# Even rows of x handed over transposed, their norm applied at eviction, odd rows transposed once on chip

## The chip, the cores and the metric

The kernel runs on one core of a Trainium2 chip. The metric is the device time of one execution in microseconds, the median over runs. The engines are TensorE (PE, whose weight loads are listed as PEld), VectorE (DVE), ScalarE (ACT), GpSimd (POOL) and SyncE (SP), which here issues the DMAs. Work passes between an on-chip memory of 128 partitions and PSUM, into which TensorE writes its products.

## What is computed

A trunk of two layers on x with 2048 rows and 1024 columns: a gated MLP mixer, then a chunked attention mixer. The change lies in the first product of the first layer, which takes the normalized rows:

```python
def rms_norm(x, g):
    y = xf * lax.rsqrt(jnp.mean(xf * xf, axis=-1, keepdims=True) + EPS)
    return (y * g.astype(jnp.float32)).astype(x.dtype)

def gmlp_mixer(h, w_in, ln_g, ln_b, w_s, b_s, w_out):
    u, v, z = jnp.split(h @ w_in, 3, axis=-1)
    ...
    return y @ w_out

h = rms_norm(x, a_norm_g[i])
x = x + gmlp_mixer(h, a_w_in[i], ...)
```

The root of a row is one number for the whole row, so it can be multiplied onto the row's results as well as onto its inputs; the gain g belongs to a column of x.

## The kernel before

**The products.** `h @ w_in` is 2048x1024 by 1024x6144. It is cut into six passes n = 0 to 5 over the columns of w_in, and each pass is computed as a two-by-two block product with seven multiplications instead of eight. The rows are sixteen blocks of 128; pair j (0 to 7) consists of the even block 2j, called `ha[j]`, whose halves of columns are a11 and a12, and the odd block 2j+1, called `hb[j]`. The seven multiplications are phases, in the order 1, 2, 6, 5, 7, 4, 3. Phase 1 multiplies a11 by a quarter of the weights, phase 2 multiplies a12 by another; the other phases take a11, b2 and sums and differences of the halves.

**A step** is one (n, phase, j): a stationary operand S (128 rows transposed, 512 deep, in two parts, a rounded one and the rest) against a moving operand T of the weights, also in two parts. A product is four times three matmuls of 128x512 (`mm3`, L111 to L113), accumulated in one of four PSUM banks (`P`). Pass 0 does phases 1 and 2 for pass 1 too, from the same S, so these sixteen steps have 24 matmuls and pass 1 has only the other five phases. After pass 5 a part "o" follows, which multiplies by w_out, and after that the attention half.

**The order.** `run_steps` walks a list of steps. While step s is multiplied, S of step s+3 is prepared (LOOK = 3). A table, `ts` and `events`, says at which step a load, a sum on POOL or another side job is issued. Every engine works through its own queue in the order that results, and so does SP: a DMA that has to wait there holds up the ones behind it.

**S in pass 0.** `block_norm` loads a block's rows, squares and sums them on ACT (L703), adds EPS on DVE (L709), takes the power -1/2 on POOL (L710) and multiplies rows by root and gain on DVE (L714). `s_split` transposes four 128x128 pieces on TensorE into PSUM (L611), rounds them into S on ACT (L434) and writes the rest on DVE (L437). S is then stored to the tensor `hsd` (L614), and in the later passes `s_load` reads it back, 512 KB a step. `block_c` and `block_d` transpose and split two tiles of the odd rows and form the sums on POOL.

**Eviction.** `evict` copies a phase 1 product to the tile `x` on ACT (L574) and adds it into phase 2's product on DVE (`c`, L570); `x`, `y`, `c`, `d` and the scratch tile of the Square come from one pool of 25 buffers (tag "acc").

## Time and profile before

| what | before |
|---|---|
| median of 3 runs | 2657.55 us (2655.72 to 2660.52) |
| the profiled execution's span, first to last instruction | 2652.0 us |
| mean granted TensorE clock | 0.996 |
| TensorE matmuls, busy | 12960, 98% of the span |
| DVE, ACT, POOL busy | 71%, 49%, 34% |
| DMA | 718.72 MB, 271 GB/s |
| pass 0 (phases 1, 2, then the other five) | 10.82 to 71.70, to 123.02, to 242.13 us |
| pass 1 (five phases) | 242.13 to 350.93 us |

What lies between the span and the time of a run, about 5.5 us, is outside the first and the last instruction. Busy shares are unions over the instructions of an engine; a matmul counts from its start to its modelled end, so neighbours overlap, and the time that one takes in a full row of matmuls is read from the length of a stretch over their number. A wait is put down to the instruction that came last before the waiting one could start.

### The profile page before, as it was taken

The page shows a single profiled execution, that of the slowest core. Times are in us where ns is not written, and L with a number is a line of the kernel's source. Part 1 is how long each engine was busy: PE and PEld are TensorE (multiplying, and loading weights), DVE is VectorE, ACT ScalarE, POOL GpSimd, SP SyncE. Part 2 cuts the span into 40 slices and gives each one's busy share as a digit, 9 for nine tenths or more (in the row PEclk, how much of TensorE's full clock was granted, in tenths as well). Part 3 has the DMA queues.
Part 4 walks back from the last instruction along what each step waited for, and adds up shares of the span by engine and source line. Part 5 has one row for each costly group of instructions (what it writes and reads, how often), then busy time and mean ns, then how long its engine had stood idle before and what let it go on. Part 6 is the DMA issues. An engine that isn't in the chain of part 4 may idle for free. (4 is left out here: it accounts for less than half of the span.)

```text
span 2652.0 us, 37980 instructions
## 1 busy us (share of the span) xinstructions
PE 2608.0 (98%) x12960; PEld 2181.4 (82%) x12960; DVE 1885.1 (71%) x2944; ACT 1303.2 (49%) x2303; POOL 897.2 (34%) x874
## 2 busy tenths in 40 slices
PE   8999999999999999999989999999999999999997
PEld 7888888888888888888878878888888888888886
DVE  5655676865767667757767767777778777877677
ACT  5422243442533434343356456666666655666564
POOL 3611334142152322203234434344332232332245
PEclk9999999999999999999999999999999999999999
DMA  7898998989989869967776597778787666875667
GB/s 286 313 344 329 346 370 323 323 323 338 330 302 313 308 233 324 331 206 270 280 251 214 186 280 229 231 245 263 252 270 254 226 204 224 255 230 161 195 224 251
DMA packets 273856, 718.72 MB, mean 271 GB/s; under 512 B 28800, under 2 KB 68736, under 8 KB 273664
## 3 DMA queue, kind: packets, MB, share of 16 engines
q1 hardware_dynamic: 273664, 716.31, 78.4%
q8 instruction: 103, 1.69, 0.3%
q14 instruction: 89, 0.73, 0.1%
HBM read 531.12 MB, written 174.59 MB: 266 GB/s over the span
## 5 line engine op out<-in xcount | busy, mean ns | idle before, releaser
L111 PE MATMUL P<-T,S 128*128 128x512 f32 x1248 | 496.2, 398 | 2.1 <-ACT S L434 2.1
L112 PE MATMUL P<-T,S 128*128 128x512 f32 x1248 | 488.2, 391 | 1.1 <-DVE T L437 1.1
L113 PE MATMUL P<-T,S 128*128 128x512 f32 x1248 | 488.6, 391 | 0.0
L1417 POOL TENSOR_SCALAR pr<-pr,sl 128x640 f32<-128x640 f32 (+4 forms) x256 | 209.7, 819 | 530.4 <-DVE sl L1416 445.2
L111 PE MATMUL pj<-hh_b,wh_b 128*128 128x512 f32 x768 | 320.4, 417 | 0.0
L113 PE MATMUL pj<-hh_b,wl_b 128*128 128x512 f32 x768 | 305.0, 397 | 1.2 <-DVE wl_b L229 1.1
L112 PE MATMUL pj<-hl_b,wh_b 128*128 128x512 f32 x768 | 303.4, 395 | 0.1
L1413 ACT ACTIVATE pr<-pr,nm 128x640 f32<-128x640 f32 (+4 forms) x256 | 195.5, 764 | 188.1 <-DVE nm L1406 186.6
L113 PEld LDWEIGHTS P<-T,S 128*128 128x128 f32 x1248 | 234.9, 188 | 50.5
L111 PEld LDWEIGHTS P<-T,S 128*128 128x128 f32 x1248 | 235.5, 189 | 46.9 <-ACT S L434 2.3
L112 PEld LDWEIGHTS P<-T,S 128*128 128x128 f32 x1248 | 235.6, 189 | 46.1 <-DVE T L437 1.3
L1438 DVE TENSOR_TENSOR pt<-tp,pt 128x640 fp32r<-128x640 f32 (+4 forms) x256 | 188.4, 736 | 43.7 <-ACT pt L1437 41.1
L1406 DVE CUSTOM_DVE_ANT_0 pr<-s,bias 128x640 f32<-128x640 f32 (+4 forms) x256 | 187.9, 734 | 35.7 <-PE s L1398 29.8
L1437 ACT CAST pt<-tp 128x640 fp32r<-128x640 f32 (+4 forms) x256 | 159.0, 621 | 54.0 <-PE tp L1433 49.8
L1433 PE MATMUL tp<-ident,pr 128*128 128x128 f32 x1120 | 166.7, 275 | 8.6 <-DVE pt L1438 7.3
L113 PEld LDWEIGHTS pj<-hh_b,wl_b 128*128 128x128 f32 x768 | 144.7, 188 | 36.4 <-DVE wl_b L229 3.8
L1433 PEld LDWEIGHTS tp<-ident,pr 128*128 128x128 f32 x1120 | 130.7, 140 | 43.3 <-issue 13.7
L111 PEld LDWEIGHTS pj<-hh_b,wh_b 128*128 128x128 f32 x768 | 145.8, 190 | 18.1 <-ACT wh_b L228 1.6
L1458 PEld LDWEIGHTS pv<-pt,V 128*128 128x128 f32 x896 | 143.3, 189 | 20.8 <-DVE pt L1438 3.9
L112 PEld LDWEIGHTS pj<-hl_b,wh_b 128*128 128x128 f32 x768 | 145.8, 190 | 17.1 <-DVE hl_b L186 0.6
L1458 PE MATMUL pv<-pt,V 128*128 128x256 f32 (+3 forms) x896 | 154.5, 320 | 2.2 <-ACT pt L1437 1.1
L229 DVE TENSOR_TENSOR wl_b<-raw_b,wh_b 128x1024 fp32r<-128x1024 f32 x96 | 120.4, 1255 | 28.5 <-ACT wh_b L228 27.8
(294 smaller groups left out, 5725.9 us busy)
## 6 DMA issues: line engine op xcount, KB each, us to landing
S<-hsd SPq DMA_DIRECT2D x288, 512.0 KB, 5.3
rw<-in_w_a SPq DMA_DIRECT2D x108, 512.0 KB, 6.3
A<-ytd SPq DMA_DIRECT2D x72, 512.0 KB, 5.7
raw_b<-wk SPq DMA_DIRECT2D x72, 512.0 KB, 4.3
hsd<-S SPq DMA_DIRECT2D x56, 512.0 KB, 4.9
V<-vhd SPq DMA_DIRECT2D x56, 512.0 KB, 5.4
bias<-reld SPq DMA_DIRECT2D x64, 320.0 KB, 4.2
va<-vd SPq DMA_DIRECT2D x32, 512.0 KB, 5.5
```

What stands on the lines that cost most here:

```text
L111: first = mm(ps, lh, rh, start=first, stop=False)
L112: mm(ps, lh, rl, start=False, stop=False)
L113: mm(ps, ll, rh, start=False, stop=last)
L229: tv(wl[:], raw[:], wh[:].bitcast(F32), op=sub)
L1406: nc.vector.tensor_tensor_reduce(out=pr[:, c0:].rearrange("p (a b) -> p a b", a=nseg), in0=ps[:, :nseg, :w], in1=bias[:, c0:].rearrange("p ...
L1413: nc.scalar.activation(pr[:, c0:], pr[:, c0:], AF.Exp, scale=-1.0, bias=nm[:], accum_out=sl[:])
L1417: nc.gpsimd.tensor_scalar(pr[:, c0:], pr[:, c0:], sl[:], 1.0, op0=ALU.mult, op1=ALU.mult)
L1433: ins = tpose(tp[:, b, :], pr[:, b * P : (b + 1) * P], ident[:])
L1437: nc.scalar.copy(oh, tp[:, b0:5, :].rearrange("p a b -> p (a b)"))
L1438: nc.vector.tensor_tensor(pt[:, 2560 + o + b0 * P : 2560 + o + 640], tp[:, b0:5, :].rearrange("p a b -> p (a b)"), oh.bitcast(F32), op=ALU ...
L1458: mm(po[:, q0 * P : q1 * P], vtl[t, p][:, i, hs], rhs, start=(i == blocks[0] and j == 0), stop=(i == 7 and j == 1),)
```

## The change

The host hands over x a second time, transposed in each block (`xt`), and the gain as 128x8 (`a_norm_gt`, on chip `ga`).

- Phases 1 and 2 take the even rows as the host transposed them: `s_gain` multiplies four pieces of 128x128 by the gain, once on ACT and once on DVE for the rest, and the root is multiplied on at eviction from `rs`. In pass 0 the tile is `ha[j]`, in passes 2 to 5 it is a tile `xq` of 256 KB, loaded for each step instead of S. S of phases 1 and 2 is no longer stored.
- The even rows' roots come from a second load of these rows, as rows, into `xr`, one buffer for all eight blocks. The root is stored to `rsd`, read back spread over the partitions (`rb`), and multiplied onto the transposed `ha[j]` together with the gain (`x_scale`, 128x128 pieces on DVE) for the phases that need sums.
- Odd rows are normalized as rows as before; then `row_turn` transposes the whole block once (eight pieces) and ACT copies it back over the rows. Sums on POOL are taken of transposed tiles, so `s_split` transposes nothing, and S of phase 7 is split from `h21` at its step, not stored and loaded again in pass 0.
- The "acc" pool has 23 buffers instead of 25, and takes the `xq` tiles too.

In all TensorE has 160 matmuls fewer (64 transposes are left of 224), ACT 320 instructions more, DVE 360 more, POOL as many as before, SP 9 DMAs more; the DMAs move 24.1 MB less. The attention half differs only in that two one-column tiles became one of two columns.

```diff
@@ evict, phases 1 and 2 (not for the step "o")
-                nc.scalar.copy(xa[n, j][:], ps[:])
+                nc.scalar.mul(xa[n, j][:], ps[:], rs[:, 2 * j : 2 * j + 1])
...
-                tt(c[:], ps[:], xa[n, j][:], op=add)
+                    last["evict"] = nc.vector.scalar_tensor_tensor(
+                        c[:], ps[:], rs[:, 2 * j : 2 * j + 1], xa[n, j][:], op0=mul, op1=add
+                    ).ins.name
@@ s_split: no transposes inside, the source is already turned
-            pt = ptp[0].tile([P, 4, P], F32, tag="t0", name=f"t0_{ph}_{j}", bufs=4)
-            for k in range(4):
-                tpose(pt[:, k, :], rows[:, k * P : k * P + P], ident[:])
             t = s_tile(f"S0_{ph}_{j}")
-            split(t[:, 0], t[:, 1], pt[:], "S")
+            split(
+                t[:, 0].rearrange("p k c -> p (k c)"), t[:, 1].rearrange("p k c -> p (k c)"),
+                rows, "S",
+            )
@@ new
+        def s_gain(n, ph, j, rows):
+            t = s_tile(f"S{n}_{ph}_{j}")
+            for k in range(4):
+                r_ = rows[:, k * P : k * P + P]
+                g_ = ga[:, 4 * (ph - 1) + k : 4 * (ph - 1) + k + 1]
+                in_order("S", nc.scalar.mul(t[:, 0, k], r_, g_))
+                nc.vector.scalar_tensor_tensor(
+                    t[:, 1, k], r_, g_, t[:, 0, k].bitcast(F32), op0=mul, op1=sub
+                )
+            return s_views(t)
+        def xq_load(n, ph, j):
+            t = xq[n, ph, j] = acc_tile(f"xq{n}_{ph}_{j}")
+            nc.sync.dma_start(t[:], xt[2 * j, :, (ph - 1) * 512 : ph * 512])
@@ acc_tile
-            return ca.tile([P, 512], F32, tag="acc", name=name, bufs=25)
+            return ca.tile([P, 512], F32, tag="acc", name=name, bufs=23)
@@ block_norm, block_a and block_b are replaced by
+        def x_load(j):
+            h = ha[j] = p0.tile([P, D], F32, tag="ha", name=f"ha{j}", bufs=8)
+            nc.sync.dma_start(h[:], xt[2 * j])
+        def row_load(blk):
+            if blk % 2:
+                t = hb[blk // 2] = p0.tile([P, D], F32, tag="hb", name=f"hb{blk // 2}", bufs=3)
+            else:
+                t = rows_[blk] = p0.tile([P, D], F32, tag="xr", name=f"xr{blk}", bufs=1)
+            nc.sync.dma_start(t[:], x[blk * P : (blk + 1) * P, :])
+        def row_root(blk):
...
+            ins = nc.scalar.activation(junk, t, AF.Square, scale=1.0 / 32, accum_out=r)
...
+            nc.vector.tensor_scalar(r, r, EPS, None, op0=add)
+            ins = nc.gpsimd.tensor_tensor(r, r, mhalf[:], op=ALU.pow)
+        def row_store(blk):
+            nc.sync.dma_start(rsd[blk][:], rs[:, blk : blk + 1])
+        def row_spread(blk):
+            b = rbc[blk] = p0.tile([P, P], F32, tag="rb", name=f"rb{blk}", bufs=4)
+            nc.sync.dma_start(b[:], rsd[blk][:].rearrange("a b -> (a b)").partition_broadcast(P))
+        def x_scale(j, ks):
...
+                nc.vector.scalar_tensor_tensor(
+                    h_, h_, ga[:, k : k + 1], b[:], op0=mul, op1=mul
+                )
+        def row_scale(j):
...
+            nc.vector.scalar_tensor_tensor(t, t, r, gab[:], op0=mul, op1=mul)
+        def row_turn(j):
...
+            for k in range(KD):
+                tpose(half[k // 4][:, k % 4, :], t[:, k * P : (k + 1) * P], ident[:])
+            for h in range(2):
+                nc.scalar.copy(
+                    t[:, h * 512 : h * 512 + 512], half[h][:].rearrange("p k c -> p (k c)")
+                )
@@ prep0
-                return s_split(1, j, a11)
+                return s_gain(0, 1, j, a11)
-                return s_split(2, j, a12)
+                return s_gain(0, 2, j, a12)
...
+            if ph == 7:
+                return s_split(7, j, h21.pop(j)[:])
@@ the table of steps
+        for j in range(NJ):
+            e = 2 + j * 12 // 7
+            if j:
+                put(j - 4, x_load, j)
+            for i, f_ in enumerate((row_load, row_root, row_store, row_spread)):
+                put(j - 3 + i, f_, 2 * j)
+            put(j + 2, x_scale, j, range(4))
...
+            put(j + 22, x_scale, j, range(4, 8))
+            put(e - 1, row_load, 2 * j + 1)
+            put(e, row_root, 2 * j + 1)
+            put(e + 1, row_scale, j)
+            at(e + 3, lambda j=j: row_turn(j))
...
@@ prep_in
+            if ph in (1, 2):
+                return s_gain(n, ph, j, xq.pop((n, ph, j)))
             return s_load(ph, j, n)
```

Three places show how the instructions stand. A row gives the line, the operation, what it writes and reads, the shape, and in brackets the engines or DMA queues whose signal it waits for; numbers at the end of a name are buffers.

The first is TensorE's queue at the start of pass 0, behind the warm-up products `wp`. P_1_0 is the product of phase 1, pair 0; S_1_0 its stationary operand; `t` a transposed piece in PSUM. Before:

```order
L879 MATMUL wp<-wz 128x256 x32
L611 MATMUL t_1_0_394<-ident,ha_377 128x128 x4
L111 MATMUL P_1_0_482<-T_1_00_406,S_1_0_399 128x512
L611 MATMUL t_1_1_443<-ident,ha_379 128x128 x4
L112 MATMUL P_1_0_482<-T_1_01_407,S_1_0_399 128x512
L113 MATMUL P_1_0_482<-T_1_00_406,S_1_0_399 128x512
L111 MATMUL P_1_0_482<-T_1_00_406,S_1_0_399 128x512
```

and now:

```order
L937 MATMUL wp<-wz 128x256 x32
L117 MATMUL P_1_0_453<-T_1_00_395,S_1_0_382 128x512
L118 MATMUL P_1_0_453<-T_1_01_396,S_1_0_382 128x512
L119 MATMUL P_1_0_453<-T_1_00_395,S_1_0_382 128x512
L117 MATMUL P_1_0_453<-T_1_00_395,S_1_0_382 128x512
L118 MATMUL P_1_0_453<-T_1_01_396,S_1_0_382 128x512
```

The transposes ahead of and between the first products are gone.

The second is SP's queue from the first load for phase 2's weights (`rw_2`) on. Before:

```order
L470 DMA rw_2_100_636<-in_w_a 128x1024 [waits DMAHW0_49]
L697 DMA hb_640<-in_x 128x1024 [waits DMAHW1_49]
L614 DMA hsd_5_204<-S_1_5_633 128x1024 [waits DMAHW2_49,DVE_49]
L614 DMA hsd_1_224<-S_4_1_650 128x1024 [waits DMAHW3_49,DVE_49]
L470 DMA rw_2_101_698<-in_w_a 128x1024 [waits DMAHW4_49]
L470 DMA rw_2_100_700<-in_w_a 128x1024 [waits DMAHW5_49]
L614 DMA hsd_6_205<-S_1_6_695 128x1024 [waits DMAHW6_49,DVE_49]
L614 DMA hsd_0_231<-S_5_0_709 128x1024 [waits DMAHW7_49,DVE_49]
L470 DMA rw_2_101_757<-in_w_a 128x1024 [waits DMAHW0_49]
L697 DMA hb_759<-in_x 128x1024 [waits DMAHW1_49,PE_49,Pool_49]
```

and now:

```order
L736 DMA xr_550<-in_x 128x1024 [waits DMAHW1_49,Activation_49]
L476 DMA rw_2_100_593<-in_w_a 128x1024 [waits DVE_49]
L736 DMA hb_603<-in_x 128x1024 [waits DMAHW3_49]
L756 DMA rb_605<-rsd_162 128x128 [waits DMAHW7_49,DMAHW4_49]
L752 DMA rsd_164<-rs 128x1 [waits DMAHW5_49,Pool_49]
L736 DMA xr_611<-in_x 128x1024 [waits DMAHW6_49,Activation_49]
L729 DMA ha_613<-in_xt 128x1024
L476 DMA rw_2_101_654<-in_w_a 128x1024 [waits DMAHW0_49,DVE_49]
L476 DMA rw_2_100_656<-in_w_a 128x1024 [waits DMAHW1_49,DVE_49]
L756 DMA rb_667<-rsd_164 128x128 [waits DMAHW5_49,DMAHW2_49]
L752 DMA rsd_166<-rs 128x1 [waits DMAHW3_49,Pool_49]
L736 DMA xr_673<-in_x 128x1024 [waits DMAHW4_49,Activation_49]
```

The stores of S (`hsd`) have left this stretch; loads of `xr`, each waiting for ACT's Square of the block before, the transposed tiles `ha`, and the small transfers of roots stand in it instead, the loads of `rw_2` among them.

The third is DVE's queue in pass 2, around the first evictions of phase 2 (`c_0`, `c_1`). `va` are tiles of the spatial gating and `T_6` weights of phase 6. Before:

```order
L808 SCALAR_TENSOR_TENSOR va_0_2_3409<-va_0_2_3409,lrs,lb_3135 128x512 [waits DVE_49]
L437 TENSOR_TENSOR vl_0_2_3559<-va_0_2_3409,vh_0_2_3558 128x1024 [waits PE_49,Activation_49]
L437 TENSOR_TENSOR T_6_01_3626<-ch_3467,T_6_00_3625 128x1024 [waits PE_49,Activation_49]
L570 TENSOR_TENSOR c_0_3536<-P_2_0_3523,x_0_3323 128x512 [waits PE_49]
L437 TENSOR_TENSOR T_6_11_3648<-ch_3467,T_6_10_3647 128x1024 [waits Activation_49]
L570 TENSOR_TENSOR c_1_3576<-P_2_1_3563,x_1_3352 128x512 [waits PE_49]
L807 SCALAR_TENSOR_TENSOR va_0_3_3521<-va_0_3_3521,lmv,lg_3134 128x512 [waits DMAHW3_49]
```

and now:

```order
L866 SCALAR_TENSOR_TENSOR va_0_2_3447<-va_0_2_3447,lrs,lb_3106 128x512 [waits DVE_49,Pool_49]
L640 SCALAR_TENSOR_TENSOR S_2_2_3586<-xq_2_2_3497,ga,S_2_2_3586 128x128 [waits DMAHW0_49,Activation_49]
L640 SCALAR_TENSOR_TENSOR S_2_2_3586<-xq_2_2_3497,ga,S_2_2_3586 128x128 [waits Activation_49] x3
L640 SCALAR_TENSOR_TENSOR S_2_3_3614<-xq_2_3_3537,ga,S_2_3_3614 128x128 [waits DMAHW1_49,Activation_49]
L866 SCALAR_TENSOR_TENSOR va_0_2_3447<-va_0_2_3447,lrs,lb_3106 128x512 [waits DVE_49]
L640 SCALAR_TENSOR_TENSOR S_2_3_3614<-xq_2_3_3537,ga,S_2_3_3614 128x128 [waits Activation_49] x3
L443 TENSOR_TENSOR T_6_01_3734<-ch_3523,T_6_00_3733 128x1024 [waits PE_49,Activation_49]
L587 SCALAR_TENSOR_TENSOR c_0_3612<-P_2_0_3599,rs,x_0_3327 128x512 [waits PE_49]
L640 SCALAR_TENSOR_TENSOR S_2_4_3663<-xq_2_4_3569,ga,S_2_4_3663 128x128 [waits DMAHW5_49,Activation_49]
L865 SCALAR_TENSOR_TENSOR va_0_3_3595<-va_0_3_3595,lmv,lg_3105 128x512 [waits DMAHW6_49]
L640 SCALAR_TENSOR_TENSOR S_2_4_3663<-xq_2_4_3569,ga,S_2_4_3663 128x128 [waits Activation_49] x2
L587 SCALAR_TENSOR_TENSOR c_1_3661<-P_2_1_3648,rs,x_1_3365 128x512 [waits PE_49]
```

Around the same evictions now stand the pieces of S_2_2 to S_2_4, four for each step, which wait for the load of `xq` and for ACT's half of the same piece.

117 lines of the change are left out of this document (59 added, 58 removed).

## The prediction

> **What bounds the kernel now.** First the page's busy times, then who TensorE waits for in the first 1100 us, then the stages of the first pass over the rows, cut at each stage's first product.
>
> ```profile
> PE 2608.0 (98%) x12960; PEld 2181.4 (82%) x12960; DVE 1885.1 (71%) x2944; ACT 1303.2 (49%) x2303; POOL 897.2 (34%) x874
> engine line waited for: us in total, times, longest us
> PE t L611 <- DVE hb L714: 4.0, 1, 4.0
> PE P L111 <- ACT S L434: 2.1, 1, 2.1
> PE wp L879 <- POOL wz L876: 1.3, 1, 1.3
> PE P L112 <- DVE T L437: 1.1, 1, 1.1
> PE t L611 <- DVE ha L714: 0.4, 1, 0.4
> PE t L611 <- DVE ra L709: 0.3, 1, 0.3
> 10.82:71.70 60.88, 55.42 (x261) 45.35 (x261) 38.47 (x48) 34.81 (x62) 25.65 (x25) 0.94 0.77 290
> 71.70:123.02 51.32, 51.32 (x264) 43.10 (x262) 35.21 (x53) 24.88 (x42) 37.46 (x29) 1.00 0.85 306
> 123.02:242.13 119.11, 119.11 (x567) 98.37 (x566) 75.22 (x108) 37.66 (x59) 20.27 (x16) 1.00 0.95 340
> 242.13:350.93 108.80, 108.80 (x481) 90.09 (x480) 65.60 (x100) 24.41 (x34) 27.09 (x19) 1.00 0.94 349
> ```
>
> The columns of a window are its length and the busy time of PE, PEld, DVE, ACT and POOL, then the granted clock, the DMA share and GB/s. TensorE is the bound. From 52 us to the end of the gMLP half it waits for nobody, so there an instruction taken off it is time gained and one put on another engine costs nothing until that engine runs out. Before 52 us it waits 9.2 us in all. The last two windows hold 480 products' matmuls each, so 108.80/480 = 0.2267 us is one 128x512 matmul, and a two-product step of 24 is 5.44 us. The first window, with its 192, should take 43.5 and takes 60.9.
>
> **The change, part by part.** *160 transposes go (224 to 64).* These are all of them, and those of the third window alone:
>
> ```profile
> L611 PE MATMUL t<-ident,ha x128: 270/272/328, 8.1 to 233.8; 128*128 128x128 f32 x128
> L611 PE MATMUL t<-ident,hb x64: 272/273/447, 28.5 to 123.0; 128*128 128x128 f32 x64
> L611 PE MATMUL t<-ident,h x32: 270/272/273, 147.3 to 170.1; 128*128 128x128 f32 x32
> ...
> L611 PE MATMUL t<-ident,ha 128*128 128x128 f32 x52 | 7.8, 272 | 0.0
> L611 PE MATMUL t<-ident,h 128*128 128x128 f32 x32 | 4.8, 272 | 0.0
> L611 PE MATMUL t<-ident,hb 128*128 128x128 f32 x3 | 0.5, 272 | 0.0
> ```
>
> A duration of 272 ns is pipelined. The price is the difference of two windows with equal products: (119.11 - 108.80)/87 = 0.118 us each; in the second window (51.32 - 43.52)/71 = 0.110. With 0.113, 160 of them are **-18.1 us** (17.6 to 18.9). Even rows lose 128, the h tiles 32; the odd rows keep 64, eight per block instead of four for each of two tiles.
>
> *The start.*
>
> ```profile
> 0.72 1.28 ACT L703 ACT_TABLE_LOAD   x1 [0.72 <-PEq L1986]
> 4.33 1.06 ACT L703 ACTIVATE jk<-ha 128x1024 bf16<-128x1024 f32 x1 [2.33 <-DMA ha<-in_x]
> 6.76 1.28 DVE L714 SCALAR_TENSOR_TENSOR ha<-ha,ra,gab 128x1024 f32<-128x1024 f32 x1 [1.09 <-DMA gab<-in_a_norm_g]
> 8.10 0.66 PE L611 MATMUL t<-ident,ha 128*128 128x128 f32 x4 [0.40 <-DVE ha L714]
> 9.24 1.04 ACT L434 CAST T<-rw 128x1024 fp32r<-128x1024 f32 x1
> 10.19 0.58 ACT L434 CAST S<-t 128x512 fp32r<-128x512 f32 x1
> 10.82 0.50 PE L111 MATMUL P<-T,S 128*128 128x512 f32 x1 [2.07 <-ACT S L434]
> ```
>
> Square, root, scale, transpose and split stand between the landing at 4.33 and the first product at 10.82. In the change ACT has there the table load (1.28), which now waits for the small ga transfer right behind ha, four multiplies by the gain (0.3 each, started back to back) and the first weight cast (1.04). With ga landed at 5.0 that is 5.0 + 1.28 + 1.2 + 1.04 = 8.5, so **-2.3 us**; landing as late as gab, which stood second before, at 6.76, it is 10.3 and -0.5. I take the early end, since ga has 4 KB and gab 512. The 1.1 us wait for the weights' low part stays.
>
> *The hole at 47 us.* The first odd blocks' loads, queued behind eight even loads and the stores, left TensorE without work:
>
> ```profile
> 47.34 1.07 ACT L703 ACTIVATE jk<-hb 128x1024 bf16<-128x1024 f32 x1
> 48.30 0.20 ACT L703 ACTIVATION_READ_ACCUMULATOR jk<-hb 128x1 f32 x1
> 51.10 1.09 PE L611 MATMUL t<-ident,hb 128*128 128x128 f32 x4 [4.04 <-DVE hb L714]
> 47.59:51.00 3.41, 0.00 (x0) 0.00 (x0) 2.74 (x6) 3.41 (x8) 0.56 (x1) 1.00 1.03 422
> 51.00:54.41 3.41, 3.31 (x10) 2.86 (x11) 2.56 (x4) 2.60 (x4) 3.22 (x3) 0.50 1.03 418
> ```
>
> Now block j's odd rows are turned three steps after their root, and no transpose stands before a product that needs it soon: -4.0 -0.3. An empty window of 3.41 us was followed by one at clock 0.50, which lost half of itself: -1.7. Together **-6.0 us** (0 if a new hole takes its place).
>
> *The even rows' roots: a new wait.* The rows are loaded a second time into one buffer, xr, so a load waits on SP for the Square of the block before, and the transposed tile, the weights of phase 2 and the spreads are queued behind it on SP; S of step 6 sits behind that load, and its product behind S. One block's cycle c is a landing and a Square (1.07 + 0.20). The landings that the first pass shows, in 52:72, over the whole pass, and in 36:52:
>
> ```profile
> hb<-in_x SPq DMA_DIRECT2D x2, 512.0 KB, 4.0
> hb<-in_x SPq DMA_DIRECT2D x8, 512.0 KB, 6.6
> hb<-in_x SPq DMA_DIRECT2D x2, 512.0 KB, 7.2
> vd<-x SPq DMA_DIRECT2D x8, 256.0 KB, 6.3
> ```
>
> So c is 5.3 to 8.5; I take 6.6, from the middle of 4.0 and 6.6, since fewer stores share the queue. The first xr is the seventh transfer, its Square done near 13. S of step 6 is ready at 13 + 4c + a landing + 1.5 = 13.2 + 5c, wanted at 8.5 + 1.7 (the cold clock of before) + 6 x 5.44 + 8 turns x 0.113 = 43.7. At 6.6 it comes at 46.2, 2.5 late; step 7 at 13.2 + 6c = 52.8 against 52.5. **+2.8 us** (0 at c = 5.3, +14 at 8.5). Roots themselves are wanted only at eviction, with four PSUM banks before it.
>
> *S made from xq instead of loaded, phases 1 and 2 of passes 2 to 5.* Per step a 512 KB load becomes one of 256 KB plus four 128x128 multiplies on ACT and four on DVE. Their engines in pass 3, in the stretches where these S are made, and the nearest prices:
>
> ```profile
> 512.00:536.80 24.80, 24.80 (x123) 20.48 (x122) 18.79 (x24) 11.23 (x19) 7.19 (x4) 1.00 0.87 313
> 536.80:561.50 24.70, 24.70 (x122) 20.87 (x121) 15.32 (x20) 11.77 (x20) 8.57 (x6) 1.00 0.96 351
> L1438 DVE TENSOR_TENSOR pt<-tp,pt 128x128 fp32r<-128x128 f32 x16 | 4.6, 285 | 0.3
> L1413 ACT ACTIVATE pr<-pr,nm 128x128 f32<-128x128 f32 x16 | 6.4, 402 | 9.6 <-DVE nm L1406 9.5
> L714 DVE SCALAR_TENSOR_TENSOR hb<-hb,ra,gab x8: 1283/1286/2302, 27.1 to 108.0; 128x1024 f32<-128x1024 f32 x8
> ```
>
> ACT: 11.8 + 32 x 0.402 = 24.6 of 24.7, at the edge. DVE: 18.79 + 32 x 0.285 = 27.9 of 24.8, then 15.32 + 9.1 = 24.4 of 24.7: 3.1 us behind. S is made three steps (8.2 us) ahead and four banks take late evictions, so TensorE should see little: I take **+1.0 us** for the four passes (0 to 10). The lighter DMA (0.87 to 0.96 now) gains nothing where nothing waits for it. The Trainium skill's page VectorE: DVE Perf Modes, section The TRN2 errata, speaks against the change here: it wants tiles of 512 elements and more, since each instruction pays a fixed latency; its formula makes a 128x128 (58 + 128)/0.96 = 194 ns on VectorE, an estimate below the 285 of the row; by it DVE would be at 25.0 of 24.8, and the sum the same.
>
> *The rest.* The scale by the root at eviction rides on the same ACT and DVE instructions: 0. The attention half has TensorE's instructions in the same order: 0.
>
> **The sum.** -18.1 - 2.3 - 6.0 + 2.8 + 1.0 = -22.6. The profiled execution has a span of 2652.0; the median of the runs is 2657.55, so 5.5 lie around it, which I leave. Span about 2629.4, time **2635**.
>
> **Rivals.** (A) *The single row buffer paces the first pass.* For it: the landing of 7.2 in the very stretch. Against it: the queue then was full of stores that are gone. At c = 8.5 the stalls are 14 instead of 2.8, and a hole may bring back a cold window (1.7): 2646 to 2648; with a c of 10 (an 8.7 landing) steps 6 and 7 are 19.5 and 3.5 late: 2657.
>
> (B) *DVE becomes the bound in phases 1 and 2, and the kernel is slower.* Its new multiply reads two SBUF tiles, as L714 does, whose slowest took 2302 ns where the median is 1286, 1.8 times, when POOL worked beside it. At 1.8 x 0.285 = 0.51 us each, 64 of them are 32.6 where the two stretches leave 6.0 + 9.4 = 15.4: 17 behind, less the 8.2 ahead, 9 us a pass, 36 in four: 2670. It flips the sign from (23.6/4 + 8.2 + 15.4)/64 = 0.46 us on. Against it: POOL is busy in only 30% of these stretches, which gives 0.285 x 1.25 = 0.36 us and 7.4 behind, inside the lead. The Trainium skill's GPSIMD Engine Reference, Specifications, says that GpSimd shares its SBUF interfaces with VectorE when that has two SBUF inputs; L714's slow ones agree.
>
> (C) *Two buffers fewer.* The accumulator pool has 23 slots for sixteen x and eight y, so an eviction at the end of phase 7 waits for a store, 6.3 us after its issue in the row above, with DVE behind it: up to 6 to 15 us once, 2641 to 2650.
>
> **How the numbers follow.** Forecast, 2627 to 2644: 0.55. A: 0.20 (0.11 of it still faster, 0.07 same, 0.02 slower). B: 0.15. C, alone or with A: 0.10 (0.06 faster, 0.04 same). "Same" is within 0.2% (5.3 us), about what a measurement of this kernel can tell from no change. Faster 0.72, same 0.11, slower 0.17. The low end takes every wait at nothing (2631) and 4 us for a shorter cold start; the high end takes in A whole and leaves B out: 2627 to 2658.
>
> **What would show it.** The first product near 8.5; 64 transposes, all before 110 us; no 4 us hole at 47; waits of TensorE for S of steps 6 and 7 that sum to about 3; passes 2 to 5 as long as before though DVE is near full in their first two phases; the first pass's five last phases at 108.8, without the 10.3 more of before. I am wrong if TensorE waits more than 10 us in the first pass, or if a later pass is longer by over 2 us.

## The result and the profile after

The changed kernel takes 2756.38 us (median of four runs, 2753.66 to 2759.22) where the kernel before took 2656.85 in the same four rounds (2655.72 to 2660.52): 1.0376 times as long, 95% interval 1.0361 to 1.039. The forecast was 2635. The profiled execution took 2756.05 and has a span of 2754.3, which is 102.3 more than before. Between the time and the span of one and the same execution lie 1.7 to 2.5 us in this case's runs; the 5.5 us of the description before and of the forecast compare two executions, so the forecast's span of 2629.4 stands for about 2631 rather than 2635.

First the busy times of the whole span, then the same windows as in the prediction, cut at the stages' first products: phases 1 and 2 of the first pass (pass 0), its other five phases, pass 1, pass 2 and pass 3. The last two rows are passes 2 and 3 of the kernel before. Columns are the window and its length, the busy time of PE, PEld, DVE, ACT and POOL, the granted clock, the DMA share and GB/s.

```profile
PE 2624.4 (95%) x12800; PEld 2177.5 (79%) x12800; DVE 2026.9 (74%) x3304; ACT 1398.2 (51%) x2623; POOL 921.5 (33%) x874
8.15:82.70 74.55, 56.00 (x209) 42.91 (x209) 31.37 (x72) 39.15 (x80) 9.27 (x13) 0.84 0.94 181
82.70:153.38 70.68, 56.41 (x234) 44.86 (x232) 62.89 (x90) 37.97 (x78) 37.05 (x29) 0.88 0.64 206
153.38:277.53 124.15, 112.86 (x489) 91.78 (x488) 100.52 (x149) 43.48 (x69) 44.79 (x31) 0.99 0.88 319
277.53:388.84 111.31, 109.36 (x481) 89.94 (x480) 65.12 (x102) 26.41 (x42) 25.91 (x19) 1.00 0.94 344
388.84:576.00 187.16, 174.96 (x821) 142.97 (x820) 147.40 (x218) 86.94 (x180) 70.34 (x46) 0.99 0.78 290
576.00:764.51 188.51, 177.78 (x836) 146.90 (x834) 139.67 (x209) 85.77 (x176) 68.89 (x42) 0.97 0.79 274
```

```profile
350.93:521.29 170.36, 170.36 (x821) 142.57 (x820) 120.78 (x153) 67.39 (x109) 62.10 (x44) 1.00 0.91 335
521.29:693.24 171.95, 171.95 (x836) 143.85 (x834) 115.74 (x144) 68.00 (x111) 59.43 (x41) 1.00 0.92 327
```

| us of span | start | pass 0 | pass 1 | pass 2 | pass 3 | pass 4 | pass 5 | rest |
|---|---|---|---|---|---|---|---|---|
| before | 10.82 | 231.32 | 108.80 | 170.36 | 171.95 | 171.95 | 171.95 | 1605.49 |
| after | 8.15 | 269.38 | 111.31 | 187.16 | 188.50 | 187.48 | 185.44 | 1607.31 |

"Rest" goes to the start of TensorE's last matmul; 9.4 and 9.5 us follow it. Two places hold the loss: pass 0 has 38.1 more, passes 2 to 5 have 62.4 more. Pass 1 has 2.5 more, 2.0 of it TensorE's wait for two loads of S. The reader should see in pass 0 that TensorE's busy time did not fall although nearly all of the 160 transposes are gone from it: 56.00 + 56.41 + 112.86 = 225.3, against 55.42 + 51.32 + 119.11 = 225.9 before. The idle time rose from 5.5 to 44.1, and the clock in the first two windows is 0.84 and 0.88, where before it was 0.94 and 1.00. So the 18 us saved came back as slower matmuls, and 38.6 us of idle time came on top. Passes 2 to 5 lose in the same two ways: 42.1 us are idle time, 20.3 are more busy time for the same matmuls, at a clock of 0.97 to 0.99. In passes 3 to 5 all of the loss lies in phases 1 and 2, the ones whose S is now made from xq: in pass 3 they take 28.9 and 37.2 us instead of 24.8 and 24.7, and the other five take what they took before. In pass 2 it lies behind phase 1, half of it in phase 6 (33.4 instead of 24.7).

The waits of TensorE say for what. The first five rows are the longest up to the end of pass 0, the next four those of passes 2 to 5 (in which it waited for nothing before); each has the total, the times and the longest in us.

```profile
PE P L117 <- ACT S L639: 15.5, 5, 6.5
PE t L778 <- DVE hb L770: 12.8, 5, 4.6
PE t L778 <- ACT S L639: 4.2, 1, 4.2
PE P L118 <- DVE T_hl L443: 4.0, 1, 4.0
PE P L118 <- DVE T L443: 3.8, 2, 3.0
...
PE mx L118 <- DVE vl L443: 10.9, 4, 3.9
PE ty L900 <- ACT yo L902: 7.5, 4, 2.9
PE P L117 <- DVE c L587: 6.8, 6, 2.1
PE ty L900 <- DVE y L920: 4.6, 3, 2.5
```

In pass 0 it is the S of phase 1 (made by L639 from the transposed tile) and the scaled odd rows; in passes 2 to 5 it is mostly DVE, in the spatial gating (`mx`, `vl`, `ty`, `y`) and at the evictions (`c`), hardly the new S itself (2.8 us for L640).

Why S came late in pass 0 is in ACT's timeline (start, length, operation, and in brackets the idle time and its releaser). These are the first Square of an xr buffer, the sixth, and S of step 6 behind it:

```profile
12.38 1.06 ACT L745 ACTIVATE xr<-xr 128x1024 f32<-128x1024 f32 x1 [0.23 <-DMA xr<-in_x]
...
62.57 1.06 ACT L745 ACTIVATE xr<-xr 128x1024 f32<-128x1024 f32 x1 [6.71 <-DMA xr<-in_x]
...
64.09 1.28 ACT L639 ACTIVATE S<-ha,ga 128x128 fp32r<-128x128 f32 x4
```

Five cycles take 50.2 us, 10.0 each. In 0:90 the DMA issues show where they go (KB each, median us to landing), and the packets' line how small the pieces are:

```profile
DMA packets 6862, 16.20 MB, mean 180 GB/s; under 512 B 2250, under 2 KB 3018, under 8 KB 6858
...
xr<-in_x SPq DMA_DIRECT2D x8, 512.0 KB, 9.6
rb<-rsd SPq DMA_DIRECT2D x6, 64.0 KB, 6.2
rsd<-rs SPq DMA_DIRECT2D x8, 0.5 KB, 10.4
```

A store of one block's 128 roots, 512 bytes in all, takes 10.4 us to land, longer than the 512 KB beside it. In the first window the DMA engines are taken to 94% while they move 181 GB/s; in the window of the same phase before, 77% moved 290.

For passes 2 to 5, the new multiply of DVE, its durations (min, median, max) and its group (busy us, mean ns, and the idle time before it); then one moment of pass 2 at which POOL adds two 128x512 tiles:

```profile
L640 DVE SCALAR_TENSOR_TENSOR S<-xq,ga,S x256: 284/343/1390, 387.5 to 1007.8; 128x128 fp32r<-128x128 f32 x128
L640 DVE SCALAR_TENSOR_TENSOR S<-xq,ga,S 128x128 fp32r<-128x128 f32 x256 | 123.0, 528 | 13.9 <-ACT S L639 13.8
...
570.20 3.39 POOL L451 TENSOR_TENSOR ch<-rw,rw 128x512 f32<-128x512 f32 x2 [10.83 <-DMA ytd<-yo]
572.37 1.37 DVE L640 SCALAR_TENSOR_TENSOR S<-xq,ga,S 128x128 fp32r<-128x128 f32 x1
```

The mean, 528 ns, lies above the 0.46 us at which the prediction's rival B flips the sign. The slowest do not take 1.8 times as long but 1.05 us more, four times the 0.343 of the median: 1.37 us for 128 elements a partition while POOL works. Of the 256, 48 run over 0.5 us, and every one of the 48 ends 0.145 to 0.153 us behind the end of a POOL addition: it waits until that addition is over.

### The profile page after: what moved, and what is told of

Read it like the earlier page. It is cut to its first block, busy times and chain, and to the rows that moved or that the text cites. A ratio compares the mean times of both kernels' runs of the same rounds, so it can differ in the third digit from the quotient of the medians.

```text
span 2754.3 us, 38402 instructions
## 1 busy us (share of the span) xinstructions
PE 2624.4 (95%) x12800; PEld 2177.5 (79%) x12800; DVE 2026.9 (74%) x3304; ACT 1398.2 (51%) x2623; POOL 921.5 (33%) x874
## 5 line engine op out<-in xcount | busy, mean ns | idle before, releaser
L117 PE MATMUL P<-T,S 128*128 128x512 f32 x1248 | 504.2, 404 | 39.2 <-ACT S L639 15.5
L119 PE MATMUL P<-T,S 128*128 128x512 f32 x1248 | 497.0, 398 | 2.8 <-DVE S L640 2.8
L118 PE MATMUL P<-T,S 128*128 128x512 f32 x1248 | 495.8, 397 | 3.8 <-DVE T L443 3.8
L1478 POOL TENSOR_SCALAR pr<-pr,ns 128x640 f32<-128x640 f32 (+4 forms) x256 | 206.1, 805 | 528.9 <-DVE ns L1477 450.9
L117 PEld LDWEIGHTS P<-T,S 128*128 128x128 f32 x1248 | 240.4, 193 | 94.5 <-ACT S L639 17.2
L1474 ACT ACTIVATE pr<-pr,ns 128x640 f32<-128x640 f32 (+4 forms) x256 | 195.5, 764 | 196.2 <-DVE ns L1467 195.3
L119 PEld LDWEIGHTS P<-T,S 128*128 128x128 f32 x1248 | 239.5, 192 | 60.2 <-DVE S L640 8.3
L118 PEld LDWEIGHTS P<-T,S 128*128 128x128 f32 x1248 | 240.6, 193 | 50.6 <-DVE T L443 4.8
L1494 PE MATMUL tp<-ident,pr 128*128 128x128 f32 x1120 | 166.6, 274 | 12.8 <-DVE pt L1499 10.6
L118 PEld LDWEIGHTS pj<-hl_b,wh_b 128*128 128x128 f32 x768 | 145.1, 189 | 16.2
```

Of the source, the lines that this page charges most:

```text
L117: first = mm(ps, lh, rh, start=first, stop=False)
L118: mm(ps, lh, rl, start=False, stop=False)
L119: mm(ps, ll, rh, start=False, stop=last)
L1474: nc.scalar.activation(pr[:, c0:], pr[:, c0:], AF.Exp, scale=-1.0, bias=nm, accum_out=sl)
L1478: nc.gpsimd.tensor_scalar(pr[:, c0:], pr[:, c0:], sl, 1.0, op0=ALU.mult, op1=ALU.mult)
L1494: ins = tpose(tp[:, b, :], pr[:, b * P : (b + 1) * P], ident[:])
```

## The experiments

The theories the runs were to tell apart. For pass 0: the way of the roots through memory (small stores and spreads) holds up the queue; or the single xr buffer does; or too few accumulator buffers. For passes 2 to 5: the low parts that DVE now writes beside POOL; or ACT's four multiplies; or the loads of xq on SP's queue and in the accumulators' slots. Each run below is one profiled execution unless its text says otherwise; the kernel before took 2654.6 to 2656.5 beside them. Every pass named is from the trace, cut at the same products. Eight of these kernels (the one after, low_one, low_stats, low_wide, no_low, act_copy, xq_shared, xq_own) run the same pass 0, and took 266.4 to 273.4 us for it; the three with the same passes 2 to 5 (after, no_trip, no_store) took 741.7 to 748.6 for these. So differences below 7 us in either are not read as effects, unless they come with a wait that explains them.

**S stored once and loaded again (s_loaded).** Pass 0 makes S of phases 1 and 2 as in the change, but stores it; passes 2 to 5 load it as before.

```diff
-            for ph in range(3, 8) for j in range(NJ)
+            for ph in range(1, 8) for j in range(NJ)
@@ s_gain
+            later(1, lambda: paced(nc.sync.dma_start(hsd[ph, j][:], ...t...)))
@@ prep_in
-            if ph in (1, 2):
-                return s_gain(n, ph, j, xq.pop((n, ph, j)))
             return s_load(ph, j, n)
```

> S of phases 1 and 2 is stored in pass 0 and loaded in passes 2 to 5, as in the kernel before; the first pass stays as changed, with 16 stores more. If making S on chip (multiplies on ACT and DVE, or the late xq loads) is what made passes 2 to 5 longer by 16 to 17 us each, they come back to 170 to 172 us, and the time falls by about 65 us to 2690. Rival: the smaller accumulator pool (23 for 25) holds these passes up; then they stay near 187 us and the time near 2756.

It took 2704.2. Passes 2 to 5 are 170.24, 172.00, 171.91 and 171.79, the times of before; pass 0 grew from 269.4 to 279.6 by the sixteen stores, 10 more than was allowed for. The window of pass 3:

```profile
568.62:740.62 172.00, 171.97 (x835) 143.68 (x834) 118.19 (x144) 68.69 (x111) 59.20 (x41) 1.00 0.93 326
```

TensorE is busy in 171.97 of 172.00. So the whole 62 us of the later passes come with S made of xq, and nothing of them from the 23 accumulator buffers alone, which this kernel has too.

**Low parts from one tile (low_one).** In passes 2 to 5 DVE writes zero times the high part instead of the true low part, so that it reads one tile.

```diff
+                if n:
+                    nc.vector.tensor_scalar(t[:, 1, k], t[:, 0, k].bitcast(F32), 0.0, None, op0=mul)
+                    continue
```

> In passes 2 to 5 the low part of S is left out: DVE writes zero times the high part, in as many 128x128 instructions at the same place and with the same waits, but each reads one tile instead of two. Port theory: DVE instructions with two SBUF inputs lose about 1.03 us whenever they meet a POOL instruction; these no longer do, their longest stays under 0.5 us instead of 1.39, and passes 2 to 5 get shorter by 10 to 16 us each: 2695 to 2715. Queue theory: xq comes late because SP is held up, and ACT and DVE then run late whatever the form; the passes stay at 185 to 188 us, and the time at 2745 to 2756.

It took 2738.2; the passes are 180.5, 181.6, 183.2 and 181.4, between the two theories. It separates nothing, because this form too is held up:

```profile
L641 DVE TENSOR_SCALAR S<-S x256: 207/216/1333, 390.9 to 992.1; 128x128 fp32r<-128x128 f32 x128
```

Its median is 216 ns and its slowest 1333: 1.12 us more, though it reads one tile and not two. That POOL holds up only instructions with two SBUF inputs is thus refuted.

**Statistics instead of low parts (low_stats).** Four instructions that read 128 columns each and write six numbers stand in place of the multiplies in passes 2 to 5; the products use the high part twice.

```diff
+                if n:
+                    nc.vector.bn_stats(sx[:], t[:, 0, k].bitcast(F32))
+                    continue
...
+            if n:
+                return [(t[:, 0, k, :], t[:, 0, k, :]) for k in range(4)]
```

> In passes 2 to 5 the low part of S is left out and the products take the high part in its place; DVE runs four statistics instructions of 128 columns at the same places instead, which read one tile and wait for ACT as the multiplies did. Statistics showed no lengthening beside POOL (0.69 us with and without), while the zeroing of the run before did (0.22 to 1.33). Port theory: none of these exceeds 0.5 us, and passes 2 to 5 fall from 185 to 188 us to 172 to 177 each, the time to 2695 to 2715. Queue theory (xq late behind SP) or load on ACT: they stay at 180 us or above as with the zeroing, the time above 2730.

```profile
L642 DVE BATCH_NORM_STATS2 sx<-S x256: 234/285/297, 386.0 to 969.0; 128x6 f32<-128x128 f32 x128
559.17:738.87 179.70, 175.01 (x836) 144.67 (x834) 135.64 (x206) 86.91 (x176) 60.47 (x43) 0.99 0.83 288
```

The second row is its pass 3. It took 2718.36. No instruction of this form ran over 297 ns, although more than 90 of the 256 ran within a POOL addition, and pass 2 came back to 171.4. But passes 3 to 5 are 179.7, 178.7 and 178.9, between the two theories: what POOL does to DVE explains pass 2 whole and the others in part, 40 us of the 62 in all.

**One wide low part (low_wide).** One 128x512 subtraction of the high part from xq replaces the four multiplies in passes 2 to 5 (the gain is left out of the low part).

```diff
+            if n:
+                nc.vector.tensor_tensor(t[:, 1]..., rows[:], t[:, 0]...bitcast(F32), op=sub)
```

> In passes 2 to 5 the four low-part multiplies of a step become one 128x512 subtraction of two tiles (the gain is left out of its first operand). If a meeting with POOL costs about 1.03 us an instruction whatever its size, a quarter of the instructions meets a quarter as often: the lengthening per step falls from 4 x 0.19 to about 0.25 us, and passes 2 to 5 fall to 173 to 178 us, the time to 2700 to 2720. If the cost goes with the bytes that are read (1.8 times, as the prediction priced it), the wide form is lengthened as much in all and the passes stay at 181 us or above.

```profile
L646 DVE TENSOR_TENSOR S<-xq,S x64: 623/682/1816, 394.4 to 992.0; 128x512 fp32r<-128x512 f32 x64
```

It took 2740.78, with passes of 177.0, 180.0, 183.7 and 183.0. The instruction loses 1.13 us at its slowest, as much as one a quarter of its size; that the price is paid for each meeting fits. The means fit too: 960 ns against the median of 682 is 0.28 us a step, where about 0.25 was expected, and the four small ones lose 4 x (528 - 343) = 0.74. The passes gained less than expected, so as a test of the passes it is inconclusive: something beside DVE was at work.

**No low part at all (no_low).** DVE does nothing for S in passes 2 to 5; the high part is used twice.

```diff
+                if n:
+                    continue
...
+            if n:
+                return [(t[:, 0, k, :], t[:, 0, k, :]) for k in range(4)]
```

> In passes 2 to 5 DVE does nothing for S of phases 1 and 2 (the low part is left out, the products take the high part twice); ACT's four multiplies a step and the xq loads stay. DVE theory: what the statistics run left (7 us a pass in passes 3 to 5) is DVE's plain time, 32 x 0.26 us a phase, so these passes come to 170 to 174 us and the time to 2685 to 2697. ACT or queue theory: the ACT multiplies or the late xq are what is left, the passes stay at 177 to 180 us and the time at 2710 to 2720.

It took 2723.0. Pass 2 is 170.29, but passes 3 to 5 are still 182.8, 182.9 and 179.5, two of them above either theory. First its pass 3; then what ACT waits for and what DVE's first operation of the spatial gating waits for in passes 2 to 5, and last that same wait of DVE in the passes of before:

```profile
557.69:740.53 182.84, 175.85 (x836) 145.48 (x834) 116.38 (x145) 86.61 (x177) 59.00 (x42) 0.98 0.82 281
...
ACT S L639 <- DMA xq<-in_xt: 38.0, 24, 6.4
DVE va L869 <- DMA va<-vd: 70.7, 12, 10.8
```

```profile
DVE va L807 <- DMA va<-vd: 20.4, 10, 3.6
```

DVE's busy time is that of before (116.4 against 115.7), and yet 11 us are missing. ACT waits for xq for 38 us, and DVE for `va` for 70.7 us instead of 20.4. Taking DVE's part away returns 16.9 + 5.7 + 4.6 + 6.0 = 33 of the 62 (with the statistics it was 40, so the share is good to some 7 us); the other 22 to 29 are another thing.

**ACT's part alone (loaded_act).** S is stored and loaded as in s_loaded, and ACT still does four 128x128 multiplies, by one, in place, for each step of phases 1 and 2 of passes 2 to 5.

```diff
+                later(2, lambda: [
+                    in_order("S", nc.scalar.mul(t[:, 0, k], t[:, 0, k].bitcast(F32), 1.0))
+                    for k in range(4)])
```

> S of phases 1 and 2 is stored and loaded as in the kernel before, with no xq; in passes 2 to 5 ACT still does its four 128x128 multiplies a step, by 1.0 in place over the high part, and DVE none. Theory that ACT's work is what is left of the longer passes 3 to 5 (8 to 11 us a pass without any DVE work): they stay at 180 to 183 us, the time near 2735 to 2745. Theory that xq is (it takes slots of the accumulator pool, SP waits for them with other loads behind, and ACT waits for xq in order): they come to 172 to 174 us, the time to 2704 to 2712.

```profile
581.00:754.87 173.87, 172.58 (x835) 143.53 (x834) 119.71 (x144) 79.75 (x174) 59.86 (x41) 1.00 0.90 326
```

The passes are 174.2, 173.9, 172.9 and 171.8. ACT carries its extra work (79.8 us against 68.7) for 0 to 4 us a pass; it is acquitted. The time, 2723.59, is above what was expected: pass 0 took 284.7 here, 5 more than in s_loaded, and pass 1 and what follows pass 5 took 4 more each.

**One copy on ACT (act_copy).** Passes 2 to 5 take one 128x512 copy of xq by ACT (no gain, no low part, nothing on DVE).

```diff
+            if n:
+                in_order("S", nc.scalar.copy(t[:, 0]..., rows[:]))
+                return [(t[:, 0, k, :], t[:, 0, k, :]) for k in range(4)]
```

> xq is loaded as in the change, but in passes 2 to 5 ACT makes the high part in one 128x512 copy (0.59 us, without the gain) instead of four multiplies (4 x 0.39) and DVE does nothing; the products take the high part twice. ACT-work theory: half of the ACT time goes, and passes 3 to 5 fall from 180 to 183 to 175 to 178 us, the time to about 2705. Queue theory: the wait for xq and what is queued behind it stay, and the passes stay at 179 us or above, the time at 2715 to 2723.

It took 2719.88: 170.2, 177.9, 183.7 and 178.5. Two of passes 3 to 5 came below the 179 of the queue theory. But with next to nothing left on either engine they keep 6 to 12 us each, so it is the load of xq itself, where it stands and where it lands.

**The slots of xq (xq_shared and xq_own).** Both are no_low with one buffer each, instead of two, for the spatial gating's gain and bias, to make room; xq_own also gives xq four buffers of its own instead of slots among the accumulators.

```diff
-            t = xq[n, ph, j] = acc_tile(f"xq{n}_{ph}_{j}")
+            t = xq[n, ph, j] = up[0].tile([P, 512], F32, tag="xq", ..., bufs=4)
```

> As no_low (DVE does nothing for S of phases 1 and 2 in passes 2 to 5), with one buffer instead of two for each of the two rows of layer-norm constants; xq still shares the accumulator pool. It is the other side of the next run. Passes 3 to 5 should stay at 179 to 183 us if the constants' buffers matter little; a single buffer may add up to 2 us a pass.

> As the run before, with four buffers of its own for xq, so that an xq load waits for ACT's reading of the fourth before it instead of for a slot that an eviction's store or the gating chain has to free. If the shared slots make xq late, passes 3 to 5 fall to 172 to 175 us, the time to 2690 to 2700, and ACT's waits for xq (38 us in passes 2 to 5) to under 15. If it is the wait in ACT's order as such (a load that ACT must wait for, wherever it lands), they stay within 2 us of the run before.

Pass 3 of the one and of the other, then ACT's wait for xq and DVE's for `va` in passes 2 to 5, of xq_shared first:

```profile
562.66:746.12 183.46, 175.35 (x835) 145.04 (x834) 116.80 (x145) 86.61 (x177) 59.14 (x42) 0.98 0.81 281
564.62:743.48 178.86, 174.16 (x835) 144.15 (x834) 116.18 (x144) 85.59 (x175) 55.83 (x41) 0.99 0.85 293
```

```profile
ACT S L639 <- DMA xq<-in_xt: 39.0, 21, 5.7
DVE va L869 <- DMA va<-vd: 71.9, 12, 11.1
...
ACT vh L440 <- DMA xq<-in_xt: 0.7, 1, 0.7
DVE va L869 <- DMA va<-vd: 52.4, 12, 7.1
```

xq_shared took 2728.5 and xq_own 2712.5. Passes 3 to 5 go from 183.5, 183.4 and 181.6 to 178.9, 177.8 and 172.3. With buffers of its own xq is in time (0.7 us of waiting instead of 39), which returns 20 us; less than expected, since passes 3 and 4 stay above 175. Shared slots are thus shown for more than half of what was left without DVE's part, in these kernels. The same two waits in the changed kernel itself, passes 2 to 5:

```profile
ACT S L639 <- DMA xq<-in_xt: 39.4, 14, 8.5
DVE va L865 <- DMA va<-vd: 23.6, 9, 3.5
```

The wait for xq is there in full; the wait for `va` is hardly longer than the 20.4 of before. It grows only where DVE has less to do and comes earlier, and it isn't what lengthens a pass by itself: in pass 5 of xq_own DVE waits for `va` for 10.3 us in phase 2, and this phase takes 24.8 us, as before; in loaded_act it waits 41.7 us in four passes that are 6.5 longer in all. What the 13 us are that passes 3 to 5 of xq_own have left stays open.

**The way of the roots, pass 0 (no_trip and no_store).** no_trip leaves out the stores of the roots and the spreads; the scale takes columns of the gain instead. no_store leaves out the stores alone; the spreads read the gain from memory. Both leave the roots out of the even rows of phases 3 to 7.

```diff
-            nc.sync.dma_start(rsd[blk][:], rs[:, blk : blk + 1])
+            pass
@@ no_trip
-            b = rbc[blk] = p0.tile([P, P], F32, tag="rb", ...)
-            nc.sync.dma_start(b[:], rsd[blk]...partition_broadcast(P))
+            rbc[blk] = gab[:, 0:P]
@@ no_store
-            nc.sync.dma_start(b[:], rsd[blk]...partition_broadcast(P))
+            nc.sync.dma_start(b[:], a_norm_g[0:P].partition_broadcast(P))
```

> The trip of the even rows' roots through DRAM is left out (neither the stores of 128 pieces of 4 bytes nor the spread loads; the scale takes the gain's first columns in their place). Small-transfer theory: these stores, which take 10 us to land, slow all loads behind them, and the waits of the first 180 us (some 50 us) mostly go: pass 0 falls from 269 to 215 to 235 us, the time to 2705 to 2722. Single-buffer theory: the loads of xr still wait for the Square of the block before; the cycle stays above the step, pass 0 gains less than 12 us, and the time is above 2744.

> Only the stores of the roots are left out; the spread loads read the gain's first 128 numbers instead, in the same shape and at the same places, without waiting for a store. If the stores of 4-byte pieces are the cost, this gains nearly what leaving out the whole trip gains (within 8 us of it); if the spread loads of 64 KB are, it gains less than a third of it.

| us | phase 1 | phase 2 | rest of pass 0 | pass 0 | time |
|---|---|---|---|---|---|
| before | 60.88 | 51.32 | 119.12 | 231.32 | 2656.85 |
| after | 74.55 | 70.68 | 124.15 | 269.38 | 2756.38 |
| no_trip | 49.13 | 69.75 | 122.20 | 241.08 | 2719.15 |
| no_store | 52.75 | 61.12 | 129.00 | 242.87 | 2736.97 |

Of no_trip its two windows of phases 1 and 2, its packets in 0:90 and the landing of xr:

```profile
8.48:57.61 49.13, 47.06 (x216) 38.38 (x217) 36.69 (x92) 41.65 (x87) 10.31 (x15) 1.00 0.80 288
57.61:127.36 69.75, 56.03 (x227) 44.46 (x226) 68.08 (x92) 34.73 (x71) 45.42 (x33) 0.88 0.63 215
...
DMA packets 6755, 22.47 MB, mean 250 GB/s; under 512 B 1253, under 2 KB 1253, under 8 KB 6750
...
xr<-in_x SPq DMA_DIRECT2D x8, 512.0 KB, 4.2
```

The stores cost 26.5 us of pass 0, the whole trip 28.3; that leaves pass 0 at 241, above the 215 to 235 that were expected. Eight of them are 8 x 128 = 1024 pieces of four bytes; 2250 - 1253 = 997 fewer small packets let the queue move 22.5 MB in 90 us instead of 16.2, and xr, still in one buffer, lands in 4.2 instead of 9.6. With the spreads kept and the stores alone gone, in no_store, it is

```profile
xr<-in_x SPq DMA_DIRECT2D x8, 512.0 KB, 4.5
```

That settles the single buffer: it was slow because the queue was. (More buffers for xr were not tried. no_store's time is 18 us above no_trip's, of which 11 lie behind pass 5 and 4 in pass 1; the 11 I cannot account for.)

The second window shows what is left. In phase 2 DVE is busy in 68.08 of 69.75 us, and all 13.8 us for which TensorE waits are waits for DVE (8.1 for scaled odd rows, 2.9 for weights, 2.8 at evictions): in no_trip it bounds there, and TensorE's clock in this window is 0.88. DVE now scales the even rows in pieces of 128, makes low parts from two SBUF tiles and splits the other phases' S from SBUF too.

**Roots spread by TensorE, S loaded (pe_loaded), and with less on DVE (best1).** pe_loaded is s_loaded in which TensorE turns the column of roots, repeated 128 times, into a PSUM tile (16 more transposes) that the scale reads. best1 also lets ACT put the gain on phase 2's half in place, and uses 512-wide instructions there.

```diff
-            b = rbc[2 * j]
+            b = ptp.tile([P, 4, P], F32, tag="t0", ..., bufs=4)[:, 0, :]
+            tpose(b, rs[:, 2 * j : 2 * j + 1].to_broadcast([P, P]), ident[:])
@@ best1
+            if ph == 2:
+                for k in range(4):
+                    nc.scalar.mul(r_, r_, ga[:, 4 + k : 5 + k])
+                split(t[:, 0]..., t[:, 1]..., rows, "S")
```

> S of phases 1 and 2 loaded in passes 2 to 5, and the roots spread over the partitions by a transpose on TensorE into PSUM (16 more transposes) instead of the trip through DRAM. If the two causes add, 2704 falls by what leaving out the trip gained in pass 0 (28 us) and by the extra that the stores of S cost beside the small transfers (10): 2668 to 2680, pass 0 at 240 to 246. If the stores of S are what holds pass 0 up without the trip too, pass 0 stays above 255 and the time above 2685.

> As the run before, and in phase 2 of pass 0 the gain is multiplied in place on ACT, so that DVE makes the low part in one 128x512 subtraction and the second half of the scale in one 128x512 multiply with one operand in PSUM, instead of four small ones each. If DVE, lengthened by POOL, is what bounds phases 2 and 6 of pass 0 (98% busy there), phase 2 falls from 70 to 55 to 62 us and the time to 2645 to 2662. If the odd rows' late loads are, it changes by less than 5 us.

pe_loaded took 2664.18, better than expected: pass 0 is 236.6 and passes 2 to 5 are 170.2 and three times 171.8. best1 took 2664.57: phase 2 went from 62.1 to 60.7 and pass 0 to 231.3, less than equal code scatters by, and what follows pass 0 gave it back. The roots' new way gains 43 us of pass 0 against s_loaded; the lighter phase 2 is worth little. By what was expected of it, under 5 us, best1 speaks for the late odd rows and against DVE as the bound of phase 2 in these kernels, where DVE is busy in 57.9 of 62.1 us and then 54.5 of 60.7.

**The gain on the weights (gain_t).** As pe_loaded, but in phases 1 and 2 the gain is multiplied into the weights as they are split, so S is the plain split of the tile from the host; and phase 4's S is split from the transposed piece while it is still in PSUM. Ten runs.

```diff
@@ weights of phases 1 and 2
+                        nc.scalar.mul(hi[:, c], v[:, c], g_)
+                        nc.vector.scalar_tensor_tensor(lo[:, c], v[:, c], g_, hi[:, c].bitcast(F32), op0=mul, op1=sub)
@@ prep0
-                return s_gain(0, 1, j, a11)
+                return s_split(1, j, a11)
-            s_split(4, j, b2_)
+            s_split(4, j, turned.pop(j)[:].rearrange("p k c -> p (k c)"))
```

> S of phases 1 and 2 is split from the raw transposed rows (one 128x512 cast and one subtraction), stored and loaded in passes 2 to 5; the gain is multiplied onto the weights of phases 1 and 2 when these are split (two 128x512 on ACT and DVE instead of one 128x1024); roots go through a transpose on TensorE; S of phase 4 is split from the transposed piece in PSUM instead of its copy. If DVE beside POOL bounds the first pass, pass 0 falls from 231 to 237 to 218 to 228 us, and the time to 2642 to 2656, under the kernel before; the split of phase 4 takes 0.69 us however POOL works, where the one from the copy took 1.10. If the odd rows' loads or the stores bound it, pass 0 stays at 231 or above and the time at 2658 to 2666.

It took 2656.7 (2650.18 to 2659.7) beside 2656.08 for the kernel before (13 runs), 1.0 times as long, interval 0.999 to 1.0009. It leaves nothing out, and is no faster than the kernel before. Its pass 0, and the splits of S there from SBUF (`hb`) and from PSUM (`t`), then the splits in pass 0 before, all from PSUM, and after, from SBUF:

```profile
8.24:240.29 232.05, 215.42 (x944) 173.30 (x945) 173.06 (x273) 111.90 (x188) 93.90 (x72) 0.97 0.87 321
...
L443 DVE TENSOR_TENSOR S<-hb,S 128x512 fp32r<-128x512 f32 x8 | 10.5, 1312 | 0.8 <-ACT S L440 0.6
L443 DVE TENSOR_TENSOR S<-t,S 128x512 fp32r<-128x512 f32 x8 | 5.4, 677 | 0.0
```

```profile
L437 DVE TENSOR_TENSOR S<-t,S 128x512 fp32r<-128x512 f32 x56 | 37.1, 685 | 13.0 <-ACT S L434 13.0
```

```profile
L443 DVE TENSOR_TENSOR S<-hb,S 128x512 fp32r<-128x512 f32 x16 | 14.6, 921 | 0.0
L443 DVE TENSOR_TENSOR S<-ha,S 128x512 fp32r<-128x512 f32 x16 | 13.8, 870 | 0.0
```

TensorE's busy time in pass 0 is 215.4, 10 less than before, with 140 matmuls fewer and a clock of 0.97 instead of 0.99. Pass 0 still takes 232.1, since 16.6 us of idle time stand where 5.5 stood. Expected were 218 to 228 if DVE beside POOL bounded this pass: missed; 231 or above was what the other theory said, late odd rows or stores, which no run took apart. The split from PSUM came out as expected. The same split of 128x512 takes 677 to 685 ns when the piece it reads lies in PSUM, and 870 to 1312 on the mean when it reads it from SBUF.

## Why the prediction was wrong, point by point

**The transposes (-18.1): right.** In the phase after S is all there (phase 5) nothing but 32 transposes left, and it went from 25.30 to 21.84: 0.108 each. 64 stayed, the last at 162.1 instead of before 110.

**The start (-2.3): right.** The first product began at 8.15 instead of 10.82, -2.7, and along the way that was forecast: ACT's table load began at 4.58, with `ga` landed, where 5.0 had been taken.

**The hole at 47 us (-6.0): failed.** The alternative named there, that a new hole takes its place, came true more than once: the scaled odd rows alone were waited for five times, 12.8 us. They are late without the roots' trip too (10.9 us in no_trip).

**The even rows' roots (+2.8): the form was right, its cycle was not.** With the measured c of 10.0 the formula gives S of step 6 at 13.2 + 50.0 = 63.2; ACT started it at 64.09 and had it at 65.37. With no_trip's landing of 4.2 and a Square, c is 5.5, S would come at 40.7, before the 43.7 at which it is wanted; in no_trip ACT had it at 39.50, and TensorE waited 0.4 us for S. The step that failed is "I take 6.6, from the middle of 4.0 and 6.6, since fewer stores share the queue": the change brings eight stores of its own, and no term of the sum prices them. I took a transfer's size in bytes for its size, and bounded c by landings from a queue without such stores. Rival A named what a c of 10 costs, 23 us of waits, but blamed the single buffer; phase 1 lost 25.4 against no_trip. The Trainium skill's DMA: Bandwidth & Descriptors, Specifications, has the rule that would have warned: under 512 B a transfer misses the line rate and the engine reads, modifies and writes. The lost rate agrees (1024 pieces of 4 B, 94% busy at 181 GB/s); the read and rewrite no run shows.

**A second omission in pass 0: DVE.** For pass 0 the prediction counts ACT's multiplies by the gain, but not that the splits of the other phases' S now read SBUF instead of PSUM, nor what DVE's new instructions sum to in phase 2. Phase 2 was to lose its transposes; it was 19.4 longer than before, and 18.4 longer with the trip gone and DVE 98% busy. Of the +38.1 then, -18 are transposes and +28 the trip. The other 28 lie in phases 2 and 6, which in no_trip are 18.4 and 8.5 longer than before, with DVE, the late odd rows and the lower clock in them. How much is DVE's is not shown: it bounds phase 2 in no_trip, but in best1 less work for it there gained 1.3 us.

**S from xq (+1.0, 0 to 10): failed, at +62.** The term rested on "so TensorE should see little", from engine sums. Two things were missing. First the price of a meeting with POOL: the prediction scaled L714's 1.8 as a factor. The runs show an added 1.02 to 1.13 us at the most for each meeting, whatever the instruction's size, so the factor is 4 for a 128x128. The plain price was short as well, 0.285 where the median is 0.343: its row, L1438, is of another operation and reads `tp`, which TensorE writes into PSUM. With 30% of the time POOL's, the factor 1.8 gave a mean of 0.36 us; it was 0.53. Rival B, given 0.15, took 0.51 and said 36 us in four passes; taking DVE's work away returned 33. It had the engine, the phases and the sign, but by a factor where the runs show an addition, so that its number comes this near is in part luck. Second, no rival had the loads of xq as late themselves: 256 KB in place of 512 was put down as lighter traffic, while its slots among the accumulators cost 20 us between xq_shared and xq_own, and what else is in the 22 to 29 that DVE doesn't explain stays open.

**Rival C: not seen.** In passes 2 to 5 with 23 accumulator buffers and S loaded, TensorE never waited; the pool's slots mattered only once xq took them too. **Pass 1 (not in the sum):** +2.5. **The rest (0):** +1.8, within what other runs show for that part.

The sign was wrong because the waits that were added sat on shared things (a queue, VectorE's turn beside GpSimd, the accumulators' slots), and I priced them by sums of bytes and of busy time.

## What to carry to other kernels

Price a transfer by its pieces as well as its bytes, and ask which row of the trace shows pieces that small; if none does, the landing of a large transfer is no upper bound. Before moving an operand from PSUM to SBUF, or adding small VectorE instructions beside a busy GpSimd, price each meeting as an addition of up to the length of GpSimd's instruction, whatever the size of its own, so that many small instructions are the dearest form: 256 small ones were lengthened by 47 us in all, 64 wide ones by 18. A load that gets smaller can still cost, if it takes slots that come free later.
